# Five PSUM banks for each wide pair, decay vectors made behind the second head, sigmoids one pair later, and the first sum of values behind the weights

## The chip, the cores and the metric

The kernel runs on one core of one Trainium2 chip. The metric is the device time of one execution in microseconds; lower is better. TensorE multiplies, ScalarE (ACT) and VectorE (DVE) do everything element by element and read TensorE's results out of PSUM, GpSimd (POOL) and SyncE (SP) issue transfers.

## The reference, cut to what matters

One decoder layer of width 1024 over 512 tokens in float32: a SwiGLU block, a mixer, a second SwiGLU block, each between two RMS norms. The change lies in the mixer:

```python
u = rms_norm(h, mix_norm_pre[l])
proj = u @ w_in[l]                       # (512, 8704)
q, k, v, xr, yr, gl = jnp.split(proj, splits, axis=-1)
# q, k, v: three dilation groups x four heads x 128
for g, (window, dilation) in enumerate(((128, 1), (512, 4), (2048, 16))):
    o_g, lse_g = dilated_group_attention(q[:, :, g], k[:, :, g], v[:, :, g], ...)
alpha = jax.nn.softmax(jnp.stack(lses, axis=0), axis=0)
attn = jnp.einsum('gbsh,gbshe->bshe', alpha, jnp.stack(outs, axis=0))
attn_d = attn.reshape(B, S, 512) @ w_attn_branch[l]
...
log_a = -LRU_C * gate_a * jax.nn.softplus(-a_param)     # in the recurrence
a = jnp.exp(log_a)
...
gates = jax.nn.sigmoid(gl).reshape(B, S, 2, D_MODEL)
merged = gates[:, :, 0] * attn_d + gates[:, :, 1] * rec_d
```

## The kernel before

**Split numbers.** A float32 product is made of three passes on numbers split in a high and a low half (fp32r): `split` lets ScalarE copy the high half (L302) and VectorE subtract it for the low half (L303). Weights come by transfer into one of four `raw` buffers, issued by SyncE, and are split into one of four `w8` buffers (high and low half of 1024 columns).

**Seven products.** Most large products are done in blocks of two by two with seven products instead of eight (Strassen's scheme in Winograd's form, p1 to p7). The sums of inputs and of weights that it needs are made by VectorE: those of the weights in `w_forms` (L691 to L696), those of the inputs in `forms_of` (`early`, L667 to L669; `middle`, L673; `late`). The products of p6 and p4 read an input form in the buffer `rb`, the others one in `big`.

**The order of the work.** Each engine executes its instructions in the order that a scheduler gives them when the kernel is built; the scheduler goes by priorities (`tc.high_priority`) and by the due times that it works out. `tc.issue_after(ins)` puts an instruction behind another of the same engine in that order. An instruction that must wait holds up all behind it on its engine.

**The mixer up to the gates** has these stages, one after the other:
- the values of group 0 (`values_first`), then those of groups 1 and 2 together by seven products (`values_two`, L1236 to L1238): VectorE sums weights in place (`add`, L1221) and splits them (`form`), TensorE runs p1, p2, p5, p6, p7, p3, p4, ScalarE copies partial sums from bank to bank (L1243);
- for each of four heads, three *wide pairs*, `qk`: one `seven_wide` makes the q and the k of one group and head, 128 columns each;
- `attend` of a head, whose work stands between the next head's pairs: scores (L1340 to L1366), exponentials (L1359, L1375), `exchange` of maxima and sums between partitions by a small matmul (L1383 and L1388 on VectorE, L1386 on TensorE), weighting (L1421, L1424), transposes (L1412, copied by L1415), values (L1430, L1435), split (L1437, L1438);
- four more wide pairs for the gates' columns, each with two sigmoids behind it (L1449, L1450) that write `facc`; `facc` held the scores of the heads before;
- the product with `w_attn_branch` (L315 to L317), multiplied into `facc` (L1457);
- the recurrence, at whose head the decay vectors `sp4` and `sp8`, 128 x 8, are made of `a_param` (L1484 to L1500).

**A wide pair** (`seven_wide`) runs its products into PSUM banks of 512 columns: in each, the left half holds one part and the right half another, and the result is their sum. Sums that several results share are carried on by copying a bank to another: `move` (L784, ScalarE). `fold` copies the left half (L790, ScalarE) and adds the right (L791, VectorE); `sum_of` adds twice (L797, L798, VectorE). All of these have a high priority (`EVAC`). The banks come from a ring of five, `acc`; the pair takes four of them:

```python
        product("p2", b, False)
        fold(b, g[0])
        product("p7", v, False)
        move(b, v)
        sum_of(u[1], v, c5)
        product("p3", z, False)
        sum_of(g[1], z, c6)
        product("p4", b, False)
        fold(b, u[0])
```

A product of a wide pair is four times a matmul of 512 columns (L779) and one of 256 (L780).

Of the kernel before, what the change touches and what calls it, by code (L numbers as in the profile page):

```python
# [10 lines left out]
F32 = mybir.dt.float32  # L11
F32R = mybir.dt.float32r
AF = mybir.ActivationFunctionType
ALU = mybir.AluOpType
AX = mybir.AxisListType

P = 128
# [156 lines left out]
SMALL = {}  # L174
# [9 lines left out]
def hybrid_layer(ctx: ExitStack, tc: tile.TileContext, xT: bass.AP, xN: bass.AP, wst: bass.AP,  # L184
                 first: bass.AP, rows: bass.AP, consts: bass.AP, bias: bass.AP, out: bass.AP):
    nc = tc.nc
    DVE, ACT, PE = nc.vector, nc.scalar, nc.tensor
# [10 lines left out]
    sm = first_t[:, 512:]  # L198
# [3 lines left out]
    facc = cpool.tile([P, KC, T], F32, name="facc")  # L202
# [29 lines left out]
    state = {"g": 0, "i": 0, "off": 0, "raw": None, "ahead": AHEAD, "split": None}  # L232
# [67 lines left out]

    def split(dh, dl, src):
        state["split"] = ACT.activation(dh, src, AF.Copy).ins  # L302
        DVE.tensor_sub(dl, src, dh.bitcast(F32))  # L303

    def acc_ps():
        return psum.tile([P, T], F32, name="acc", tag="acc", bufs=5)
# [452 lines left out]
        seventh(t, w, "p4", v, False)  # L759
        u0(v)  # L760

    def seven_wide(t, w, g, u, seen=lambda ap: ap):


        b, v, z, y = (acc_ps() for _ in range(4))

        def two(ps):
            return ps[:, :HB], ps[:, HB:]

        def product(p, ps, start):  # L770
            at = t[p].at
            part, cross = ps.rearrange("q (s c) -> q s c", s=2), two(ps)[1]
            if len(at(0, 0).shape) == 3:
                part = ps.rearrange("q (s b t) -> q s b t", s=2, b=2)
                cross = cross.rearrange("q (b t) -> q b t", b=2)
            for k in range(4):
                ks = slice(k * P, (k + 1) * P)
                wh, wl = w[p][:, 0, ks], w[p][:, 1, ks]
                PE.matmul(part, wh, at(BOTH, k), start=start and k == 0, stop=False, skip_group_check=True)  # L779
                PE.matmul(cross, wl, at(0, k), start=False, stop=k == 3, skip_group_check=True)  # L780

        def move(dst, src):
            with tc.high_priority(offset=EVAC):
                ACT.activation(dst, src, AF.Copy)  # L784

        def fold(ps, dst=None):
            out = tpool.tile([P, HB], F32, name="c", tag="c", bufs=CB) if dst is None else dst
            x, y_ = two(ps) if dst is None else map(seen, two(ps))
            with tc.high_priority(offset=EVAC):
                ACT.activation(out, x, AF.Copy)  # L790
                DVE.tensor_add(out, y_, out)  # L791
            return out

        def sum_of(dst, ps, c):
            x, y_ = two(ps)
            with tc.high_priority(offset=EVAC):
                DVE.tensor_add(c, x, c)  # L797
                DVE.tensor_add(dst, seen(y_), seen(c))  # L798

        product("p1", b, True)  # L800
        move(y, b)
        product("p5", z, True)
        c5 = fold(z)
        product("p6", y, False)
        move(v, y)
        c6 = fold(y)
        product("p2", b, False)
        fold(b, g[0])
        product("p7", v, False)
        move(b, v)  # L810
        sum_of(u[1], v, c5)
        product("p3", z, False)
        sum_of(g[1], z, c6)
        product("p4", b, False)
        fold(b, u[0])

    def seven(t, w, z, g, u):

# [297 lines left out]
    for k in range(KC):  # L1116
        wh, wl, raw = wts[k]
        if k == 0:

            z = hm(0)  # L1120
# [42 lines left out]
    def rec_half():  # L1163

        return kpool.tile([P, 8, T], F32R, name="rb", tag="rb")

    with ExitStack() as mx:
        tpl = mx.enter_context(tc.tile_pool(name="attn_out", bufs=1))
        apool_cm = tc.tile_pool(name="attention", bufs=1)
# [36 lines left out]
        def values_two(steps, then):  # L1206
# [11 lines left out]
            def add(dst, x, y):  # L1218
                with tc.high_priority(offset=AHEAD):
                    for d, x_, y_ in zip(*(two_of(a) for a in (dst, x, y))):  # L1220
                        DVE.tensor_add(d, x_, y_)  # L1221

            def form(src):
                with tc.high_priority(offset=AHEAD):
                    ws = [w8(), w8()]
                    for w, half in zip(ws, two_of(src)):
                        split(w[:, 0, :], w[:, 1, :], half)
                return ws
# [22 lines left out]
            b, y, z = [aux_ps(), aux_ps()], [acc_ps(), acc_ps()], [aux_ps(), acc_ps()]  # L1251
            c5, c6 = ([facc[:, i + j, :] for j in range(2)] for i in (0, 2))
            w1, w2 = form(g0), form(g1)
            steps[0]()
            add(sd, u0, u1)
            prod("p1", w1, b, True)
            copies(y, b)
            w5 = form(sd)
# [43 lines left out]
        def pair_of(key):  # L1302

            i = order.index(key)
            if i + 1 < len(order):
                forms[order[i + 1]] = w_forms(order[i + 1])
            return forms.pop(key)
# [22 lines left out]
        def attend(hd, heads):  # L1330
# [64 lines left out]
            DVE.tensor_tensor(nm, nm, st[:, 0, 2, :], op=ALU.min)  # L1395
            e = apool.tile([P, NG, 4], F32, name="e", tag="e", bufs=2)
            DVE.tensor_tensor(e, nm[:, None, :].to_broadcast([P, NG, 4]), st[:, 0], op=ALU.subtract)
            ACT.activation(e, e, AF.Exp)
            d = apool.tile([P, NG, 4], F32, name="d", tag="d", bufs=2)
            DVE.tensor_mul(d, e, st[:, 1])  # L1400
            tot = apool.tile([P, 4], F32, name="tot", tag="tot", bufs=2)
# [33 lines left out]
                PE.matmul(on[:, :, b, :], vt[0][:, j, :], t.rearrange("q (p r) -> q p r", p=4),  # L1435
                          start=False, stop=i == 6, skip_group_check=True)
            ACT.activation(attn.hi[hd], om, AF.Copy)  # L1437
            DVE.tensor_sub(attn.lo[hd], om, attn.hi[hd].bitcast(F32))  # L1438

        for hd in range(NH):  # L1440
            attend(hd, qkvs.pop(hd))
            if hd + 1 < NH:
                qkvs[hd + 1] = qk(hd + 1)


        for c in range(0, KC, 2):
            g, u = tmp("g"), tmp("u")
            seven_wide(t, pair_of(("pair", 52 + c, 53 + c)), [g[:, h] for h in HALVES], [u[:, h] for h in HALVES])
            ACT.activation(facc[:, c, :], g, AF.Sigmoid)  # L1449
            ACT.activation(facc[:, c + 1, :], u, AF.Sigmoid, scale=-1.0)  # L1450
        apool_cm.__exit__(None, None, None)
        for c in range(KC):
            ps = acc_ps()
# [5 lines left out]
    with ExitStack() as mx:  # L1459
# [15 lines left out]
        lpool = lpool_cm.__enter__()  # L1475


        def s8(name):
            return lpool.tile([P, 8], F32, name=name)
        o, w = SMALL["ap"]  # L1480
        av = sm[:, o:o + w]
        na, ex, zz, po = (s8(n) for n in ("na", "ex", "zz", "po"))
        sp8 = s8("sp8")
        DVE.tensor_scalar(na, av, -1.0, None, op0=ALU.mult)  # L1484
        DVE.tensor_tensor(ex, av, na, op=ALU.min)
        ACT.activation(ex, ex, AF.Exp)
        DVE.tensor_scalar(zz, ex, 2.0, None, op0=ALU.add)
        DVE.reciprocal(zz, zz)
        DVE.tensor_mul(zz, zz, ex)
        DVE.tensor_mul(ex, zz, zz)  # L1490
        DVE.memset(po, 1.0 / 19.0)
        for i in (17, 15, 13, 11, 9, 7, 5, 3, 1):
            DVE.tensor_mul(po, po, ex)
            DVE.tensor_scalar(po, po, 1.0 / i, None, op0=ALU.add)
        DVE.tensor_mul(po, po, zz)
        DVE.tensor_scalar(na, na, 0.0, None, op0=ALU.max)
        DVE.scalar_tensor_tensor(po, po, 2.0, na, op0=ALU.mult, op1=ALU.add)
        DVE.tensor_scalar(sp8, po, -8.0, None, op0=ALU.mult)
        sp4 = po
        DVE.tensor_scalar(sp4, po, 4.0, None, op0=ALU.mult)  # L1500

        def ip(ap):
            return ap.rearrange("q (i p) -> q p i", p=4)
# [124 lines left out]
        for i, (what, hd) in enumerate(LRU_ORDER):  # L1628
# [9 lines left out]
            def then():  # L1638
                if i + 1 < len(LRU_ORDER):
                    prepare(LRU_ORDER[i + 1])  # L1640
# [189 lines left out]
```

## Time and profile before

| what | value |
|---|---|
| median of 3 runs | 1218.15 us (1217.16 to 1218.87) |
| the profiled execution | 1217.25 us, its span 1215.4 us |
| TensorE busy | 1200.5 us (99% of the span) |
| VectorE busy | 1030.6 us (85%) |
| ScalarE busy | 835.9 us (69%) |
| TensorE's clock | full in all 40 slices |
| HBM | 119 GB/s over the span |

All times of a trace are counted from the start of the span. In a row of a timeline the first number is the start and the second the duration in us; a bracket gives the idle time of the engine before it and what ended that. Busy times of neighbouring operations overlap a little, since a duration counts an operation to its last write. In a row of the windows, the columns are the window, its length, and the busy time and instructions of TensorE, of its weight loads, of VectorE, ScalarE and GpSimd, then TensorE's clock, the transfers' share and GB/s.

### The profile page before, as it was taken

The page shows a single profiled execution, that of the slowest core. Times are in us where ns is not written, and L with a number is a line of the kernel's source. Part 1 is how long each engine was busy: PE and PEld are TensorE (multiplying, and loading weights), DVE is VectorE, ACT ScalarE, POOL GpSimd, SP SyncE. Part 2 cuts the span into 40 slices and gives each one's busy share as a digit, 9 for nine tenths or more (in the row PEclk, how much of TensorE's full clock was granted, in tenths as well). Part 3 has the DMA queues.
Part 4 walks back from the last instruction along what each step waited for, and adds up shares of the span by engine and source line. Part 5 has one row for each costly group of instructions (what it writes and reads, how often), then busy time and mean ns, then how long its engine had stood idle before and what let it go on. Part 6 is the DMA issues. An engine that isn't in the chain of part 4 may idle for free.

```text
span 1215.4 us, 18988 instructions
## 1 busy us (share of the span) xinstructions
PE 1200.5 (99%) x7306; PEld 1073.9 (88%) x7306; DVE 1030.6 (85%) x1608; ACT 835.9 (69%) x1449; POOL 26.2 (2%) x51
## 2 busy tenths in 40 slices
PE   9999999999999999999999999999999999999997
PEld 8899999999887888888889888888899999999996
DVE  7999888989789899999867899875799888889964
ACT  7567787886575676777735898834566677877763
POOL 0000000001011000000000000000100000000000
PEclk9999999999999999999999999999999999999999
DMA  7234333434634232222323342235443343433341
GB/s 265 89 102 138 114 133 121 134 115 155 239 125 126 70 113 71 96 85 81 99 75 122 122 156 87 87 122 175 154 139 109 120 136 108 136 115 129 122 173 70
DMA packets 45818, 149.77 MB, mean 123 GB/s; under 512 B 5152, under 2 KB 8608, under 8 KB 45728
## 3 DMA queue, kind: packets, MB, share of 16 engines
q1 hardware_dynamic: 38160, 131.09, 32.5%
q0 software_dynamic: 7280, 17.30, 4.3%
q8 instruction: 57, 0.93, 0.3%
q14 instruction: 33, 0.27, 0.1%
q10 hardware_dynamic: 288, 0.17, 0.0%
HBM read 138.06 MB, written 6.29 MB: 119 GB/s over the span
## 4 chain that ended last, share of the span: by engine, by line
PE 89%; DVE 5%; ACT 3%; DMA 2%; issue 1%; SPq 0%; DVEq 0%; ACTq 0%
PE acc L729 10%; PE acc L731 10%; PE acc L730 10%; PE acc L315 7%; PE acc L317 7%; PE acc L316 7%; PE acc L779 7%; PE aux L1035 4%; PE aux L1036 4%; PE aux L1037 4%; PE acc L780 3%; DVE w L303 2%; PE acc L433 2%; PE acc L432 2%; PE acc L431 2%; DMA raw<-in_w 1%
## 5 line engine op out<-in xcount | busy, mean ns | idle before, releaser
L303 DVE TENSOR_TENSOR w<-raw,w 128x1024 fp32r<-128x1024 f32 (+1 forms) x272 | 297.5, 1098 | 36.2 <-ACT w L302 35.4
L302 ACT ACTIVATE w<-raw 128x1024 fp32r<-128x1024 f32 (+1 forms) x272 | 259.7, 959 | 92.1 <-PE acc L317 44.5
L729 PE MATMUL acc<-big,w 128*128 128x256 f32 x920 | 260.4, 283 | 0.0
L731 PE MATMUL acc<-big,w 128*128 128x256 f32 x920 | 260.3, 283 | 0.0
L730 PE MATMUL acc<-big,w 128*128 128x256 f32 x920 | 260.3, 283 | 0.0
L729 PEld LDWEIGHTS acc<-big,w 128*128 128x128 f32 x920 | 176.2, 192 | 1.9
L730 PEld LDWEIGHTS acc<-big,w 128*128 128x128 f32 x920 | 176.3, 192 | 1.7
L731 PEld LDWEIGHTS acc<-big,w 128*128 128x128 f32 x920 | 176.3, 192 | 0.0
L779 PE MATMUL acc<-big,w 128*128 128x512 f32 x320 | 115.2, 398 | 0.3 <-ACT acc L784 0.3
L780 PE MATMUL acc<-big,w 128*128 128x256 f32 x320 | 90.6, 283 | 0.0
L1035 PE MATMUL aux<-w,xf 128*128 128x512 f32 x224 | 87.5, 393 | 0.6 <-ACT w L302 0.6
L1036 PE MATMUL aux<-w,xf 128*128 128x512 f32 x224 | 87.5, 391 | 0.0
L1037 PE MATMUL aux<-w,xf 128*128 128x512 f32 x224 | 87.2, 389 | 0.0
L779 PEld LDWEIGHTS acc<-big,w 128*128 128x128 f32 x320 | 60.1, 188 | 13.7 <-ACT acc L784 0.6
L303 DVE TENSOR_TENSOR w<-s,w 128x1024 fp32r<-128x1024 f32 x51 | 62.2, 1220 | 4.9 <-ACT w L302 4.8
L780 PEld LDWEIGHTS acc<-big,w 128*128 128x128 f32 x320 | 60.5, 189 | 0.1
L315 PE MATMUL acc<-xf,w 128*128 128x512 f32 (+1 forms) x168 | 59.0, 353 | 0.0
L317 PE MATMUL acc<-xf,w 128*128 128x512 f32 (+1 forms) x168 | 58.5, 349 | 0.0
L316 PE MATMUL acc<-xf,w 128*128 128x512 f32 (+1 forms) x168 | 58.5, 349 | 0.0
L302 ACT ACTIVATE w<-s 128x1024 fp32r<-128x1024 f32 x51 | 53.8, 1056 | 6.2 <-PE acc L731 3.0
L743 ACT ACTIVATE c<-acc 128x256 f32<-128x256 f32 x74 | 28.2, 384 | 40.7 <-PE acc L731 40.7
L1035 PEld LDWEIGHTS aux<-w,xf 128*128 128x128 f32 x224 | 41.9, 188 | 9.3 <-ACT w L302 1.2
(454 smaller groups left out, 2938.6 us busy)
## 6 DMA issues: line engine op xcount, KB each, us to landing
raw<-in_w SPq DMA_DIRECT2D x232, 512.0 KB, 3.5
big<-xf POOLq DMA_DIRECT2D x6, 512.0 KB, 3.4
gains<-in_rows POOLq DMA_DIRECT2D x5, 512.0 KB, 5.7
h<-in_x SPq DMA_DIRECT2D x8, 256.0 KB, 5.3
h<-in_xn POOLq DMA_DIRECT2D x4, 512.0 KB, 6.7
kept_m<-h POOLq DMA_DIRECT2D x4, 512.0 KB, 2.9
vals<-in_w SPq DMA_DIRECT2D x4, 512.0 KB, 6.1
h<-kept_m POOLq DMA_DIRECT2D x4, 512.0 KB, 5.5
```

The costliest lines, as they stand in the source:

```text
L302: state["split"] = ACT.activation(dh, src, AF.Copy).ins
L303: DVE.tensor_sub(dl, src, dh.bitcast(F32))
L315: PE.matmul(ps, wh, xh, start=first, stop=False)
L316: PE.matmul(ps, wh, xl, start=False, stop=False)
L317: PE.matmul(ps, wl, xh, start=False, stop=last)
L729: PE.matmul(ps, wh, xh, start=start and k == 0, stop=False, skip_group_check=True)
L730: PE.matmul(ps, wh, xl, start=False, stop=False, skip_group_check=True)
L731: PE.matmul(ps, wl, xh, start=False, stop=k == 3, skip_group_check=True)
L779: PE.matmul(part, wh, at(BOTH, k), start=start and k == 0, stop=False, skip_group_check=True)
L780: PE.matmul(cross, wl, at(0, k), start=False, stop=k == 3, skip_group_check=True)
L1035: PE.matmul(ps, xh, wh, start=first and j == 0, stop=False, skip_group_check=True)
L1036: PE.matmul(ps, xh, wl, start=False, stop=False, skip_group_check=True)
```

## The change

Four edits:
- `seven_wide` takes five banks instead of four, in the order b, z, y, v, o. The move behind p7 goes to the fifth, `o`, and p4 accumulates there; before, both used b, which `fold` of `g[0]` reads.
- `seven_wide` calls a function `then` behind that move, in ScalarE's order. The gate pairs use it to put a pair's two sigmoids behind the third move of the next pair; those of the last pair follow at the end.
- The decay vectors are made in `decay`, called once, after the second head's `attend`: its Exp stands behind that head's last Exp in ScalarE's order, its VectorE operations behind the split of that head's output. They live in a pool that lasts until the recurrence.
- In `values_two` the first sum (`add(sd, u0, u1)`) is put behind the low half of the last weights split before it (`state["low"]`).

```diff
     def split(dh, dl, src):
         state["split"] = ACT.activation(dh, src, AF.Copy).ins
-        DVE.tensor_sub(dl, src, dh.bitcast(F32))
+        state["low"] = DVE.tensor_sub(dl, src, dh.bitcast(F32)).ins
...
-    def seven_wide(t, w, g, u, seen=lambda ap: ap):
-        b, v, z, y = (acc_ps() for _ in range(4))
+    def seven_wide(t, w, g, u, seen=lambda ap: ap, then=lambda: None):
+        b, z, y, v, o = (acc_ps() for _ in range(5))
...
         def move(dst, src):
             with tc.high_priority(offset=EVAC):
-                ACT.activation(dst, src, AF.Copy)
+                return ACT.activation(dst, src, AF.Copy).ins
...
         product("p7", v, False)
-        move(b, v)
+        moved = move(o, v)
         sum_of(u[1], v, c5)
+        with tc.issue_after(moved):
+            then()
         product("p3", z, False)
         sum_of(g[1], z, c6)
-        product("p4", b, False)
-        fold(b, u[0])
+        product("p4", o, False)
+        fold(o, u[0])
...
+    decays = [s8(n, kpool) for n in ("po", "sp8")]
+
+    def decay(pool):
+        o, w = SMALL["ap"]
+        av = sm[:, o:o + w]
+        na, ex, zz = (s8(n, pool) for n in ("na", "ex", "zz"))
+        po, sp8 = decays
+        DVE.tensor_scalar(na, av, -1.0, None, op0=ALU.mult)
+        DVE.tensor_tensor(ex, av, na, op=ALU.min)
+        ACT.activation(ex, ex, AF.Exp)
+        DVE.tensor_scalar(zz, ex, 2.0, None, op0=ALU.add)
...
+        for i in (17, 15, 13, 11, 9, 7, 5, 3, 1):
+            DVE.tensor_mul(po, po, ex)
+            DVE.tensor_scalar(po, po, 1.0 / i, None, op0=ALU.add)
...
             w1, w2 = form(g0), form(g1)
+            low = state["low"]
             steps[0]()
-            add(sd, u0, u1)
+            with tc.issue_after(low):
+                add(sd, u0, u1)
             prod("p1", w1, b, True)
...
-            ACT.activation(e, e, AF.Exp)
+            state["exp"] = ACT.activation(e, e, AF.Exp).ins
...
-            DVE.tensor_sub(attn.lo[hd], om, attn.hi[hd].bitcast(F32))
+            state["low"] = DVE.tensor_sub(attn.lo[hd], om, attn.hi[hd].bitcast(F32)).ins
 
         for hd in range(NH):
             attend(hd, qkvs.pop(hd))
+            if hd == 1:
+                with tc.issue_after(state["exp"]), tc.issue_after(state["low"]):
+                    decay(apool)
             if hd + 1 < NH:
                 qkvs[hd + 1] = qk(hd + 1)
 
+        two = []
+
+        def gate():
+            if two:
+                c, g, u = two.pop()
+                ACT.activation(facc[:, c, :], g, AF.Sigmoid)
+                ACT.activation(facc[:, c + 1, :], u, AF.Sigmoid, scale=-1.0)
 
         for c in range(0, KC, 2):
             g, u = tmp("g"), tmp("u")
-            seven_wide(t, pair_of(("pair", 52 + c, 53 + c)), [g[:, h] for h in HALVES], [u[:, h] for h in HALVES])
-            ACT.activation(facc[:, c, :], g, AF.Sigmoid)
-            ACT.activation(facc[:, c + 1, :], u, AF.Sigmoid, scale=-1.0)
+            seven_wide(t, pair_of(("pair", 52 + c, 53 + c)), [g[:, h] for h in HALVES], [u[:, h] for h in HALVES],
+                       then=gate)
+            two.append((c, g, u))
+        gate()
...
-        na, ex, zz, po = (s8(n) for n in ("na", "ex", "zz", "po"))
...
+        sp4, sp8 = decays
```

More of the change, by code (lines that the diff above doesn't have):

```diff
@@ L1165, in rec_half, with s8 @@
         return kpool.tile([P, 8, T], F32R, name="rb", tag="rb")
+    def s8(name, pool):
+        return pool.tile([P, 8], F32, name=name)
+    decays = [s8(n, kpool) for n in ("po", "sp8")]
[8 more added lines that the diff above has]
+        DVE.tensor_scalar(zz, ex, 2.0, None, op0=ALU.add)
+        DVE.reciprocal(zz, zz)
+        DVE.tensor_mul(zz, zz, ex)
+        DVE.tensor_mul(ex, zz, zz)
+        DVE.memset(po, 1.0 / 19.0)
+        for i in (17, 15, 13, 11, 9, 7, 5, 3, 1):
+            DVE.tensor_mul(po, po, ex)
+            DVE.tensor_scalar(po, po, 1.0 / i, None, op0=ALU.add)
+        DVE.tensor_mul(po, po, zz)
+        DVE.tensor_scalar(na, na, 0.0, None, op0=ALU.max)
+        DVE.scalar_tensor_tensor(po, po, 2.0, na, op0=ALU.mult, op1=ALU.add)
+        DVE.tensor_scalar(sp8, po, -8.0, None, op0=ALU.mult)
+        DVE.tensor_scalar(po, po, 4.0, None, op0=ALU.mult)
     with ExitStack() as mx:
@@ L1475, in hybrid_layer @@
         lpool = lpool_cm.__enter__()
[L1478 to L1481, printed above, removed]
-        na, ex, zz, po = (s8(n) for n in ("na", "ex", "zz", "po"))
[L1483 to L1500, printed above, removed]
+        sp4, sp8 = decays
         def ip(ap):
```

## The prediction

> **What bounds the kernel now.** I read the page first, then the windows over the mixer's attention, then the timeline of each engine at every place where TensorE's starts lie further apart than its steady pitch.
>
> ```profile
> PE 1200.5 (99%) x7306; PEld 1073.9 (88%) x7306; DVE 1030.6 (85%) x1608; ACT 835.9 (69%) x1449; POOL 26.2 (2%) x51
> PE 89%; DVE 5%; ACT 3%; DMA 2%; issue 1%; SPq 0%; DVEq 0%; ACTq 0%
> ```
> ```profile
> 359.00:412.00 53.00, 50.52 (x225) 41.26 (x224) 47.63 (x50) 33.33 (x45) 7.93 (x16) 1.00 0.39 115
> 519.00:557.00 38.00, 38.00 (x239) 33.63 (x238) 36.44 (x79) 26.32 (x62) 0.00 (x0) 1.00 0.26 87
> ```
>
> TensorE is the bound: 1200.5 us of 1215.4, and 89% of the chain. The change adds and removes no matmul, so all it can win are TensorE's waits between the values (359 us) and the end of the gate pairs (612 us), 253 us in all. VectorE is nearly as full there (in the window of the third head 36.44 of 38 us); what is taken from TensorE's waits must not come back as VectorE's. The engine orders of the two kernels, both built, are the same outside this stretch, so a gain there should shift the rest unchanged.
>
> **Part 1, the first sum of values later.** TensorE's timeline, then VectorE's:
>
> ```profile
> 368.27 0.39 PE L1236 MATMUL aux<-w,big 128*128 128x512 f32 x1
> 369.82 0.50 PE L1237 MATMUL aux<-w,big 128*128 128x512 f32 x1 [1.16 <-DVE w L303]
> 381.51 0.61 PE L1236 MATMUL aux<-w,rb 128*128 128x512 f32 x2
> 383.44 0.50 PE L1237 MATMUL aux<-w,rb 128*128 128x512 f32 x1 [1.32 <-DVE w L303]
> ```
> ```profile
> 366.27 1.23 DVE L1221 TENSOR_TENSOR vals<-vals 128x1024 f32<-128x1024 f32 x1 [1.10 <-DMA vals<-in_w]
> 367.41 1.22 DVE L303 TENSOR_TENSOR rb<-ts,rb 128x1024 fp32r<-128x1024 f32 x1
> 368.55 4.62 DVE L303 TENSOR_TENSOR w<-raw,w 128x1024 fp32r<-128x1024 f32 x4
> 382.17 2.35 DVE L303 TENSOR_TENSOR w<-vals,w 128x1024 fp32r<-128x1024 f32 x2
> 386.71 1.22 DVE L303 TENSOR_TENSOR big<-ts,big 128x1024 fp32r<-128x1024 f32 x1
> ```
>
> Between 369.82 and 381.51 TensorE does 51 steps, 0.229 us each. So the first wait (369.82 - 368.27 = 1.55) costs 1.32, the second (the second matmul of the pair at 381.51 starts 0.23 later, 383.44 - 381.74 = 1.70) costs 1.47; each adds 0.10, since the matmul behind a wait takes 0.50 instead of 0.39. Both are waits for a low half of weights. The cause is one sum (L1221) that stands at the head of VectorE's queue and waits 1.10 us for its transfer.
>
> In the changed order the sum stands behind the four low halves of the 368.55 row, and its place is taken by p5's low half (the 386.71 row), whose inputs are long made. VectorE was free at 366.27 - 1.10 = 365.17; its pitch is 367.41 - 366.27 = 1.14; the first weights' low half starts after two steps, at 367.45 instead of 368.55. The first wait shrinks by 1.10. p6's first low half (382.17 now) comes twelve steps later, at 381.1, done at 382.3; but TensorE now finishes p5 before p6 and asks for it only at its 73rd matmul, 368.72 + 72 x 0.229 = 385.2. The second wait goes: 1.57. What is late next is p7: its input's low half comes seven steps and one short one (0.6) behind, 389.6 to 390.8, and is wanted at 368.72 + 96 x 0.229 = 390.7: with the refill I count 0.3. Gain 1.10 + 1.57 - 0.3 = **2.4 us**; bounds 1.1 (the second wait turns into others) and 2.9.
>
> **Part 2, five banks.** The last gate pair, TensorE, ScalarE, VectorE; and the first pair's wait:
>
> ```profile
> 598.15 0.28 PE L780 MATMUL acc<-big,w 128*128 128x256 f32 x1
> 599.51 0.51 PE L779 MATMUL acc<-rb,w 128*128 128x512 f32 x1 [1.08 <-ACT acc L784]
> 602.33 0.28 PE L780 MATMUL acc<-big,w 128*128 128x256 f32 x1
> 602.93 0.50 PE L779 MATMUL acc<-big,w 128*128 128x512 f32 x1 [0.32 <-ACT acc L784]
> 606.09 0.40 PE L316 MATMUL acc<-attn,w 128*128 128x512 f32 x1
> 606.52 0.50 PE L779 MATMUL acc<-rb,w 128*128 128x512 f32 x1
> ```
> ```profile
> 593.41 1.28 ACT L1486 ACT_TABLE_LOAD   x1
> 597.05 1.28 ACT L1449 ACT_TABLE_LOAD   x1
> 598.35 0.63 ACT L1449 ACTIVATE facc<-g 128x512 f32<-128x512 f32 x1
> 598.88 0.58 ACT L784 ACTIVATE acc<-acc 128x512 f32<-128x512 f32 x1
> 601.76 0.63 ACT L302 ACTIVATE w<-raw 128x512 fp32r<-128x512 f32 x1 [1.48 <-DMA raw<-in_w]
> 602.29 0.58 ACT L784 ACTIVATE acc<-acc 128x512 f32<-128x512 f32 x1
> 605.88 0.58 ACT L784 ACTIVATE acc<-acc 128x512 f32<-128x512 f32 x1 [0.54 <-DVE g L791]
> ```
> ```profile
> 598.41 0.17 DVE L1493 TENSOR_TENSOR po<-po,ex 128x8 f32<-128x8 f32 x1
> 598.61 0.17 DVE L1494 TENSOR_SCALAR po<-po 128x8 f32<-128x8 f32 x1
> 605.37 0.42 DVE L791 TENSOR_TENSOR g<-acc,g 128x256 f32<-128x256 f32 x1
> 607.84 0.41 DVE L798 TENSOR_TENSOR g<-acc,c 128x256 f32<-128x256 f32 x1
> ```
> ```profile
> 418.13 0.28 PE L780 MATMUL acc<-big,w 128*128 128x256 f32 x1
> 418.47 0.50 PE L779 MATMUL acc<-rb,w 128*128 128x512 f32 x1
> ```
>
> p4 waits at 606.52 for the move at 605.88, and ScalarE stood idle 0.54 before that move: it writes bank b, which VectorE's fold of g0 (605.37 + 0.42) still reads. TensorE loses 0.43 - 0.23 + 0.10 = 0.30. Such a wait stands before p4 in six of the sixteen wide pairs, from 418.47 (0.34 - 0.12 + 0.10 = 0.32) to 606.52, 1.88 us together. With a fifth bank the move needs only p7 and ScalarE, so it starts 0.46 to 0.54 earlier, more than the 0.2 or so that TensorE stood still. One of the six also had ScalarE busy with weights; in the changed order those stand behind the move. I take **1.5**; bounds 0.8 and 1.9. What is late next is ScalarE itself, finishing a 1.06 us weight copy when p7 ends.
>
> **Part 3, sigmoids behind a copy of the next pair, and no Exp between them.** ScalarE loads a table for Exp at 593.41 and one back for Sigmoid at 597.05; p6 of the last pair waits for the move that comes behind load and sigmoid (598.88): 599.51 - 598.15 = 1.36, less 0.12, plus 0.11: 1.35. In the changed order one load is left, behind a move. p7 of the same pair waits for the move at 602.29, which stands behind a weight copy that waited 1.48 for its transfer: 0.60 - 0.12 + 0.10 = 0.58. That copy now stands behind the last pair's third move and its two sigmoids, some 8 us after its buffer is free. Together 1.93; the deferred load delays the fold of g0 of the pair it lands in, whose bank the next p1 needs about 1 us later by my count, so I count it at nothing; if that cover is gone it costs up to the load's 1.28. Gain **1.9**, bounds 0.6 and 2.2.
>
> **Part 4, the order of the first head's softmax** is made anew by the scheduler, since all around it moves.
>
> ```profile
> 447.74 0.28 PE L780 MATMUL acc<-big,w 128*128 128x256 f32 x1
> 448.90 0.38 PE L1386 MATMUL aux<-xch,cst 128*128 128x32 f32 x2 [0.88 <-DVE xch L1383]
> ```
>
> TensorE waits 1.16 - 0.12 = 1.04 here for the exchange of maxima. In the changed order this matmul stands over a pair later, 1.7 us or so behind the point at which its input should be ready. Gain **0.9**; bounds -0.5 (the exchange, or another in the new order, waits anyway) and 1.0.
>
> **Part 5, the decay vectors in the third head's stage.** Thirty small VectorE operations and one Exp leave the gate pairs. They hid behind TensorE there except for the load of part 3. Now they stand singly between VectorE's other work while head 2's pairs run.
>
> ```profile
> 577.32 0.15 DVE L1403 TENSOR_TENSOR tot<-tot,d 128x4 f32<-128x4 f32 x1
> 577.38 1.22 DVE L303 TENSOR_TENSOR w<-s,w 128x1024 fp32r<-128x1024 f32 x1
> ```
> ```profile
> DVE c L791 <- ACT c L790: 0.8, 1, 0.8
> DVE w L303 <- ACT w L302: 0.5, 1, 0.5
> DVE qk L791 <- ACT qk L790: 0.5, 1, 0.5
> ```
>
> The second fence is VectorE's waits in 519 to 557. A small operation between large ones holds the queue for 577.38 - 577.32 = 0.06; in a chain, one needing the one before, it takes 598.61 - 598.41 = 0.20. The changed order alternates them with other work, so I take a little over the first, 0.08: 30 x 0.08 = 2.4 us, against 1.8 of waiting that can take them. **0.6 us** is lost; bounds 0 and 30 x 0.20 - 1.8 = 4.2. The Exp finds its table loaded and costs ScalarE one small step. The vectors' reader comes after 612 us.
>
> For small waits that any new order makes I take **0.5**, bounds 0 and 1.5, from the refill of 0.1 and waits of 0.2 that stand in six of sixteen pairs now.
>
> **Sum.** 2.4 + 1.5 + 1.9 + 0.9 - 0.6 - 0.5 = 5.6 us. The profiled execution took 1217.25 (span 1215.4), so 1211.65; the median shown, 1218.15, lies 0.9 above it, so **1212.6**. Two in a thousand, 2.4 us, is about what a measurement of this kernel can tell from no change.
>
> **Rivals.** *The small operations cost their full length* (0.12). If VectorE takes nothing up before a small operation has ended, each costs 0.20: 4.2 us net in place of 0.6, gain 6.7 - 4.2 - 0.5 = 2.0, **1216.2**. Against it: the rows 577.32 and 577.38. The Trainium skill, "VectorE: DVE Perf Modes", section "The DRAIN you can't avoid", says that the next operation waits until the pipe is empty, and advises fewer operations. By that rule this rival holds; the rows above disagree with it, at 0.06 against a duration of 0.15.
>
> *Exchanges take the waits over* (0.10). Each head has two; TensorE, which executes in order, stood still at one of eight. With TensorE ahead of VectorE, if four of the eight wait 0.98 (0.88 and the refill), part 4 is gone and three are added: 6.7 - 0.9 - 2.9 - 1.1 = 1.8, **1216.4**. For it: VectorE is as full as the second window says.
>
> *Slower: the bank of p5 comes round too soon* (0.08). With five of five banks per pair, p5 of the next pair takes the very bank z that p3 just filled, so it waits for VectorE's sum of g1 (607.84 + 0.41 = 608.25), 1.73 after p4's start at 606.52. Two products run from 599.51 to 602.33 + 0.12, 1.41 each, so p5 follows p4's start by p4 and p1, 2.82: the slack is 1.09. From there each tenth by which the sum comes later is a tenth lost in each of fifteen pairs. It takes 0.55 a pair, sums 1.65 later, to eat 5.6 and 2.4 more: **1220.6**. One more weight half (1.22) and a few decay operations ahead of the sum would do it; against it, the sums go ahead of weights in the queue.
>
> **How the numbers follow.** The forecast has 0.70. Its best end is 2.9 + 1.9 + 2.2 + 1.0 = 8.0, 1210.1; I set the low end at 1209.9. The first two rivals end near 1216.4; a little past them, at 1216.8, the range leaves out the slower rival (0.08) and the worse ends of the first two (about 0.1): 1209.9 to 1216.8. Faster by over 0.2%: nearly all of the forecast (0.68) and some of the first two rivals (0.10), 0.78; within 0.2%: the rest of these, 0.13; slower: 0.09.
>
> **What would show it.** Right: no wait over 0.4 us of TensorE on L303 in the values; no gap before p4; ScalarE's moves never idle behind L791; one table load in the gate pairs; the exchange of head 0 without a wait; VectorE's waits in head 2 down to almost none. Wrong, if TensorE's waits between 359 and 612 still add up to over 8 us, if p5 of a pair waits on L798, or if the exchanges wait.

## The result, and the profile after

The changed kernel takes 1211.81 us (median of 6 runs, 1210.72 to 1212.27) where the kernel before takes 1218.03 (6 runs, 1217.16 to 1218.87): a ratio of 0.9948, 95% interval 0.9935 to 0.9961, 6.2 us faster. The forecast was 1212.6. The sum came out nearly right, in part by luck: one of its terms, and a part of another, goes back to another edit than the one it stood under, and a loss of about 1 us or a little more was not in it at all.

The profiled execution took 1211.87 (span 1210.1). First the page's busy times and chain.

```profile
PE 1199.2 (99%) x7306; PEld 1073.7 (89%) x7306; DVE 1029.0 (85%) x1608; ACT 832.4 (69%) x1447; POOL 26.1 (2%) x51
PE 88%; DVE 6%; ACT 3%; DMA 2%; issue 1%; DVEq 0%
```

These shares hardly moved. The waits did: TensorE's between 359 and 612 us, before (first fence) and after (second). The columns are engine, tile and line, then what was waited for, the total in us, how often, and the longest.

```profile
PE aux L1237 <- DVE w L303: 2.5, 2, 1.3
PE acc L779 <- ACT acc L784: 1.4, 2, 1.1
PE aux L1386 <- DVE xch L1383: 0.9, 1, 0.9
```
```profile
PE aux L1372 <- DVE qk L791: 0.5, 1, 0.5
```

All three kinds are gone, and one new one of 0.5 has come. (Line numbers have moved: the second and third matmul of a step of the values, L1237 and L1238, are now L1267 and L1268, the exchange L1418, the sigmoids L1486 and L1487.) The values and the new wait, TensorE; then VectorE in front of the values:

```profile
368.23 0.39 PE L1266 MATMUL aux<-w,big 128*128 128x512 f32 x1
368.62 0.50 PE L1267 MATMUL aux<-w,big 128*128 128x512 f32 x1
...
418.17 0.28 PE L780 MATMUL acc<-big,w 128*128 128x256 f32 x1
418.90 0.49 PE L1372 MATMUL aux<-qk 128*128 128x128 f32 x2 [0.46 <-DVE qk L791]
```
```profile
366.21 1.22 DVE L303 TENSOR_TENSOR rb<-ts,rb 128x1024 fp32r<-128x1024 f32 x1
367.35 4.62 DVE L303 TENSOR_TENSOR w<-raw,w 128x1024 fp32r<-128x1024 f32 x4
```

The weights' low halves start at 367.35 (forecast 367.45). Of the first wait 368.62 - 368.23 - 0.23 = 0.16 is left; the second is gone.

To see where gains arise, and where they are given back, I took the start of the n-th matmul in the trace of before, less that in another trace, both counted from the first matmul at 361 us. This "lead", at points named by the time of before, with the gain of the medians (the kernels are described below):

| kernel | 410, values done | 457 | 509, two heads done | 578, third head done | 612, gates done | 705 | 841, recurrence done | gain of the median |
|---|---|---|---|---|---|---|---|---|
| changed | 2.38 | 3.25 | 3.71 | 4.26 | 6.99 | 6.86 | 6.12 | 6.22 |
| only_sum | 2.63 | 1.69 | 1.67 | 1.60 | 1.68 | 1.41 | 1.41 | 0.98 |
| only_banks | -0.03 | 1.72 | 2.39 | 2.82 | 3.11 | 3.11 | 3.11 | 2.86 |
| only_decay | -0.59 | -0.53 | -1.29 | -1.65 | 0.59 | 0.51 | -0.23 | -1.45 |
| only_sig | 0.41 | 0.38 | 0.20 | 0.28 | 0.02 | 0.02 | 0.02 | 0.04 |
| no_sum | -0.67 | 1.07 | 1.53 | 1.61 | 4.34 | 4.23 | 3.49 | 2.84 |
| no_banks | 2.41 | 1.35 | 0.56 | 0.22 | 2.54 | 2.12 | 1.38 | 1.76 |
| no_decay | 2.43 | 3.05 | 3.83 | 4.41 | 5.84 | 5.74 | 5.00 | 4.82 |
| decay_twice | 2.45 | 2.99 | 4.46 | 2.00 | 4.33 | 3.74 | 2.12 | 2.64 |
| aligned | 2.60 | 3.08 | 3.84 | 4.55 | 7.44 | 7.44 | 7.44 | 7.93 |
| shift_128 | 2.40 | 2.96 | 3.29 | 3.66 | 6.22 | 5.63 | 4.01 | 4.08 |
| only_decay_aligned | -0.10 | -0.21 | -1.22 | -1.65 | 0.58 | 0.58 | 0.58 | 0.94 |
| no_sig_aligned | 2.61 | 3.39 | 3.95 | 4.67 | 6.99 | 6.99 | 6.99 | 7.20 |

The lead at 841 us agrees with the gain of the medians to 0.7 us, but for only_decay, 1.2 off. Behind it single executions differ by up to 2 us in waits for weights (only_banks' lead falls from 3.11 to 1.03 by the last matmul, the changed kernel's from 6.12 to 5.33), so one profile's last stage says little. Where two kernels take heads in another order, a point within the heads can be off by some tenths.

The changed kernel's lead is largest at the end of the gate pairs, 6.99. Then, where no instruction was changed, it shrinks by 0.87, of which 0.74 in the recurrence. That and the waits of each edit are what the experiments are for.

### The profile page after: what moved, and what is told of

It reads as the page before. It is cut to its first block, busy times and chain, and to the rows that moved or that the text cites. A ratio compares the mean times of both kernels' runs of the same rounds, so it can differ in the third digit from the quotient of the medians.

```text
span 1210.1 us, 18990 instructions
## 1 busy us (share of the span) xinstructions
PE 1199.2 (99%) x7306; PEld 1073.7 (89%) x7306; DVE 1029.0 (85%) x1608; ACT 832.4 (69%) x1447; POOL 26.1 (2%) x51
## 4 chain that ended last, share of the span: by engine, by line
PE 88%; DVE 6%; ACT 3%; DMA 2%; issue 1%; DVEq 0%
PE acc L729 9%; PE acc L731 9%; PE acc L730 9%; PE acc L779 8%; PE acc L315 7%; PE acc L317 7%; PE acc L316 7%; PE acc L780 4%; PE aux L1037 3%; PE aux L1038 3%; PE aux L1039 3%; DVE w L303 2%; DMA raw<-in_w 2%; PE acc L433 2%; PE acc L432 2%; PE acc L431 2%
```

## Experiments: one edit at a time

Each of the four edits alone, on the kernel before.

**only_sum**

```
-            add(sd, u0, u1)
+            with tc.issue_after(low):
+                add(sd, u0, u1)
```

> The kernel before with one edit alone: the first sum of values stands behind the low halves of the second weights. Theory 1 (the parts add up: TensorE is the bound, and a wait that goes is a gain that stays): the two waits in the values at 368 and 382 us, 1.55 and 1.70, shrink to under 0.5 together; lead at the end of the values 2.4 to 2.6 us, and the time 2.4 us below before. Rival 2 (VectorE is the hidden pace-setter): the same lead at the end of the values, but VectorE, as full as before, gives over 1 us of it back in the heads by new waits of TensorE on VectorE's low halves; the time falls by under 1.4 us.

1217.02 us (11 runs), ratio 0.9990, interval 0.9981 to 0.9999: 1.0 us, not 2.4. The lead is as forecast at the end of the values, 2.63, and 0.94 less at 457. TensorE, VectorE and ScalarE of this kernel at the first pair of head 0:

```profile
415.50 0.28 PE L780 MATMUL acc<-big,w 128*128 128x256 f32 x1
416.72 0.50 PE L779 MATMUL acc<-rb,w 128*128 128x512 f32 x1 [0.94 <-ACT acc L784]
```
```profile
414.44 1.22 DVE L303 TENSOR_TENSOR w<-s,w 128x1024 fp32r<-128x1024 f32 x1
415.57 0.42 DVE L791 TENSOR_TENSOR qk<-acc,qk 128x256 f32<-128x256 f32 x1
```
```profile
416.08 0.58 ACT L784 ACTIVATE acc<-acc 128x512 f32<-128x512 f32 x1 [1.47 <-DVE qk L791]
```

Before, p4 started 0.34 after the last matmul of p7 (418.13 to 418.47); now it starts 1.22 after it. TensorE has come 2.6 us closer to VectorE, whose fold still holds bank b, and the move of that pair stands 1.47 behind it. Rival 2 holds: the gain is real, and in this kernel the next shared bank takes 0.9 of it back.

**only_banks**

```
-        b, v, z, y = (acc_ps() for _ in range(4))
+        b, z, y, v, o = (acc_ps() for _ in range(5))
...
-        move(b, v)
+        move(o, v)
...
-        product("p4", b, False)
-        fold(b, u[0])
+        product("p4", o, False)
+        fold(o, u[0])
```

> The kernel before with one edit alone: five banks in each wide pair, the move of the partial sums going to a fifth bank. Theory 1 (waits add up): the six waits before p4 go and nothing else does; 1.5 us faster, at most 1.9; the two waits of the last gate pairs (1.36 and 0.60 us, behind the table loads) stay. Rival 2: ScalarE, finishing a weight copy when p7 ends, moves no earlier, or the extra bank makes the next pair's p5 wait for VectorE's sum of g1; within 0.5 us of before, or slower, with gaps before p5.

1215.14 us (7 runs), ratio 0.9976, interval 0.9964 to 0.9987: 2.9 us, nearly twice what was expected. TensorE's waits from 407 to 612 us in this kernel, and then the exchange of head 0 on TensorE and VectorE:

```profile
PE acc L779 <- ACT acc L784: 1.5, 2, 1.1
```
```profile
453.56 0.30 PE L1386 MATMUL aux<-xch,cst 128*128 128x32 f32 x2
```
```profile
453.22 0.18 DVE L1383 TENSOR_TENSOR xch<-stn,cst 128x32 f32<-128x32 f32 x1
```

The two waits left are those of the last gate pairs. The exchange's wait of 0.9 is gone without any other edit: with the fifth bank the exchange stands at 453.56 (448.90 before), and TensorE does not wait for it. The scheduler makes this order with the fifth bank alone, so Part 4 of the forecast is a result of the banks.

**only_sig**

```
-        move(b, v)
+        moved = move(b, v)
         sum_of(u[1], v, c5)
+        with tc.issue_after(moved):
+            then()
...
-            ACT.activation(facc[:, c, :], g, AF.Sigmoid)
-            ACT.activation(facc[:, c + 1, :], u, AF.Sigmoid, scale=-1.0)
+            two.append((c, g, u))
+        gate()
```

> The kernel before with one edit alone: each gate pair's sigmoids stand behind the next pair's move. Its decay vectors are still made in the gate pairs, and with them three table loads (Sigmoid, Exp, Sigmoid). Theory 1: the table loads, and not the place of the sigmoids, made the wait of 1.36 us, so it stays or turns up at another product; the wait of 0.60 at p7 may go since its weight copy moves. 0 to 0.6 us faster. Rival 2 (the place of the sigmoids is what the waits of the gate pairs came from): both waits go without the decay vectors being moved, 1.5 to 2 us faster.

1217.96 us (11 runs), ratio 0.9999, interval 0.9991 to 1.0008: nothing. But the lead shows a gain that is lost again: 0.28 at 578 us, 1.01 at 605, 0.02 at 612. TensorE's waits from 552 to 615 us, then the second of them and the move that it waits for:

```profile
PE acc L779 <- ACT acc L784: 1.8, 2, 1.1
```
```profile
605.86 0.50 PE L779 MATMUL acc<-rb,w 128*128 128x512 f32 x1 [1.07 <-ACT acc L784]
```
```profile
605.23 0.58 ACT L784 ACTIVATE acc<-acc 128x512 f32<-128x512 f32 x1 [1.02 <-DVE g L791]
```

With the decay vectors' Exp beside the sigmoids the table is loaded three times, as before. Of the two waits of the gate pairs, the one at p6 is shorter (0.72 idle, 1.08 before) and the one at p7 is gone. A wait of 1.07 has come in front of p4, whose move must wait for VectorE's fold of the shared bank b; it takes the gain back. So theory 1 holds: the wait turns up at another product.

**only_decay**: `decay(apool)` behind the second head as in the change, its two vectors taken from `kpool`, the old code removed.

> The kernel before with one edit alone: the decay vectors' 30 small VectorE operations and their Exp stand behind the second head, in the third head's stage. Theory 1: the gate pairs keep one table load in place of three; the wait of 1.36 us at the last pair's p6 goes (gain 1.2 to 1.4), the one of 0.60 at p7, which is a weight copy waiting for its transfer, stays; the small operations cost 0 to 0.6 us in the third head; 0.8 to 1.4 us faster. Rival 2 (small operations hold VectorE for their full 0.17 to 0.20 us): 30 x 0.20 less VectorE's waits there, 1.8, so TensorE loses about 4 us in the third head and the time rises by 2 to 3 us.

1219.45 us (11 runs), ratio 1.0012, interval 1.0004 to 1.0021: slower. The stages say otherwise for the gate pairs (from -1.65 to 0.59, a gain of 2.2, more than expected, since the wait at p7 goes too). But 0.6 is lost in the values, 1.1 from 457 to 578 and 0.74 from 705 to 841. A loss in the heads was expected, though not its size. About half of it stands ahead of the first small operation, which starts at 514.87 in this kernel: the lead is -0.52 at 486 and -1.05 at 513 us. In between TensorE's order differs from that of before. The losses in the values and in the recurrence were in neither theory.

The four alone gain 0.98 + 2.86 + 0.04 - 1.45 = 2.4, together 6.2. Here the edits do not add up.

## Experiments: one edit taken out

**no_sum**, the changed kernel with `add(sd, u0, u1)` at its old place.

> The changed kernel without the edit of the first sum. Theory 1 (the parts add up): the two waits in the values are back, 1.3 and 1.5 us; the time is 2.4 to 2.6 us above the changed kernel's, so 3.5 to 4 us below before. Rival 2 (slack is shared: what one part gains, another would have given): under 1.4 us above the changed kernel.

1215.38 us (7 runs), ratio 0.9973, interval 0.9962 to 0.9984. TensorE's waits from 359 to 612 us:

```profile
PE aux L1267 <- DVE w L303: 2.8, 2, 1.5
PE aux L1417 <- DVE xch L1414: 0.2, 1, 0.2
```

Within the changed kernel the edit is worth (0.9973 - 0.9948) x 1218 = 3.0 us; alone it was worth 1.0. The leads at 841 us say 2.6 and 1.4.

The fifth bank is not what makes the difference. From 410 to 509 us the changed kernel loses 0.87 against no_sum, and only_sum lost 0.96 against before: with five banks the first matmul of the scores waits (418.90 in the changed kernel; no_sum has no such wait), with four p4 does. Of the 1.2 between 2.6 and 1.4, 0.4 arises in the values, where this kernel's two waits are 2.8 together against 2.5 before, and the rest behind 509 us; what made it there was not shown.

**no_banks**

```
-        b, z, y, v, o = (acc_ps() for _ in range(5))
+        b, v, z, y = (acc_ps() for _ in range(4))
+        o = b
```

> The changed kernel with four banks in each wide pair, the move going back into the bank of g0's fold. Theory 1: waits before p4 are back, 1.5 to 1.9 us in all, and the time is that much above the changed kernel's, 4.3 to 4.7 us below before. Rival 2: with the sigmoids and the decay vectors elsewhere, ScalarE and VectorE are early enough that p4 does not wait: within 0.7 us of the changed kernel.

1216.46 us (11 runs), ratio 0.9989, interval 0.9980 to 0.9998: (0.9989 - 0.9948) x 1218 = 5.0 us are lost, three times the expectation. The waits from 407 to 516 us (one line further down, since this version has a line more):

```profile
PE acc L780 <- ACT acc L785: 1.0, 1, 1.0
PE aux L1419 <- DVE xch L1416: 0.9, 1, 0.9
```

They are only_sum's wait in front of p4 and the exchange. The lead of 2.41 from the values falls to 1.35 at 457 and 0.22 at 578: first by what only_sum lost there, then by 1.13, which only_decay lost between the same points (1.12). With five banks the move of the decay vectors costs 0.35 there (no_decay, below). So the fifth bank removes its own waits and most of this loss; the sum's loss of 0.9 it does not remove, as no_sum shows.

**no_decay**, the changed kernel with `decay(lpool)` called where the old code was.

> The changed kernel with the decay vectors made where they were, beside the gate pairs. Theory 1: the Exp brings three table loads back into the gate pairs, a wait of 1.0 to 1.4 us with them; the small operations leave the third head, where VectorE's waits come back to 1.8 us; 0.6 to 1.4 us above the changed kernel. Rival 2 (30 small operations in the third head cost several us that other gains cover): 2 us or more below the changed kernel.

1213.40 us (5 runs), ratio 0.9962, interval 0.9948 to 0.9975: (0.9962 - 0.9948) x 1218 = 1.7 us are lost (1.1 by the leads at 841 us; the two intervals overlap). So the move of the decay vectors is worth 1 to 1.7 us in the company of the others. From 578 to 612 the lead grows by 1.43, against 2.73 in the changed kernel; from 457 to 578 by 1.36 against 1.01. So the move costs 0.35 from 457 to 578 us and brings 1.3 in the gate pairs. The lead of no_decay grows by 1.14 up to 605 us and does not fall behind it: what the sigmoids' move gains here stays with five banks, where only_sig lost it.

**decay_twice**, a second, unused set of decay vectors ahead of the first: 30 more small operations of VectorE and an Exp.

```
+    spare_decays = [s8(n, kpool) for n in ("po2", "sp82")]
...
+                    decay(apool, spare_decays)
                     decay(apool)
```

> The changed kernel with a second set of decay vectors, used by nothing, made right beside the first in the third head's stage: 30 more small VectorE operations and one more Exp. If a small operation holds VectorE for 0.08 us: 30 x 0.08 = 2.4 us more work for an engine that has few waits left there, so 1 to 2.4 us above the changed kernel, in waits of TensorE on VectorE between 510 and 550 us. If it holds VectorE for its full 0.20 us: 30 x 0.20, 4 to 6 us above. If the third head still has slack on VectorE's side: 0 to 0.5 us.

1215.58 us (11 runs), ratio 0.9978, interval 0.9969 to 0.9987: (0.9978 - 0.9948) x 1218 = 3.7 us slower than the changed kernel. That is above what 0.08 us each allows and below 0.20 each. But the lead shows two losses: one up to the third head's end, and 1.62 in the recurrence, where neither set is computed. The recurrence had to be understood first.

## Experiments: where the recurrence lost

The kernels that lose nothing between 705 and 841 us are before, only_sum, only_banks and only_sig. Those that lose 0.74 hold two decay vectors in `kpool`; decay_twice, which loses 1.62, holds four. Each is 32 bytes a partition and stands ahead of the halves of the input (rb). In the built programs rb lies at byte 147200 of a partition in the first group, at 147264 in the second, at 147328 in decay_twice; the attention output and the recurrence's tile behind it are shifted alike. TensorE's groups that read rb in the recurrence, 706 to 830 us, in the changed kernel (busy us, mean ns):

```profile
L315 PE MATMUL acc<-rb,w 128*128 128x512 f32 x36 | 14.2, 394 | 0.0
L317 PE MATMUL acc<-rb,w 128*128 128x512 f32 x36 | 14.1, 392 | 0.0
L316 PE MATMUL acc<-rb,w 128*128 128x512 f32 x36 | 14.0, 388 | 0.0
```

Before, all three rows have 389. Three explanations stood: the addresses, a slower clock after a denser stage, and decay_twice's instructions.

**aligned**, the changed kernel with the two vectors in a stretch of SBUF that holds the first weights at the start and nothing later. Instructions and their order stay; only the addresses return to those of before.

```
-    decays = [s8(n, kpool) for n in ("po", "sp8")]
+    decays = [first_t[:, 8 * i:8 * i + 8] for i in range(2)]
```

> The changed kernel, all engines' orders unchanged, with the two decay vectors (64 bytes a partition) kept in a stretch of SBUF that is dead by then, not in a tile of their own, so that the halves of the input, the attention output and the recurrence's tile lie at the addresses they had before (147200 and 163584 in place of 147264 and 163648). Theory 1 (where these tiles lie sets TensorE's pitch): the recurrence's matmuls run at 0.2267 us a step, as in the kernel before, not at 0.2267 to 0.2298; the 0.74 us lost between 705 and 841 us comes back, with 0.2 to 0.5 in the values and the output projection; 0.8 to 1.3 us below the changed kernel. Rival 2 (the chip slows TensorE because the stage before it is denser): the pitch stays, and the time with it.

**shift_128**, the same with an unused tile that shifts rb and what follows by 128 bytes.

```
+    pad = kpool.tile([P, 32], F32, name="pad")
+    DVE.memset(pad[:, :1], 0.0)
```

> The kernel 'aligned' with an unused 128 bytes a partition ahead of the input's halves, so that these tiles lie 128 bytes further on; all engines' orders the same but for one small memset. Theory 1 (addresses): steps of 0.229 and 0.237 us by turns wherever these tiles are read, 1.6 us lost in the recurrence, some 2.5 us above 'aligned'. Rival 2 (the 0.237 us in the run with two sets of decay vectors came of their 30 instructions): the same time as 'aligned'.

aligned: 1210.20 us (5 runs, 1210.05 to 1210.68), ratio 0.9940, interval 0.9926 to 0.9953. shift_128: 1214.05 us (7 runs), ratio 0.9971, interval 0.9960 to 0.9982. The two differ by 3.9 us, by addresses and one small memset alone; by the leads, 2.2 of it arises from 612 to 841 us. The windows from 706 to 830 us of before, the changed kernel, aligned and shift_128, in this order:

```profile
706.00:830.00 124.00, 124.00 (x549) 102.71 (x548) 102.83 (x135) 89.89 (x115) 1.06 (x2) 1.00 0.31 100
```
```profile
706.00:830.00 124.00, 124.00 (x546) 102.08 (x545) 100.80 (x132) 84.96 (x111) 1.06 (x2) 1.00 0.32 110
```
```profile
706.00:830.00 124.00, 124.00 (x549) 102.68 (x548) 100.44 (x131) 85.56 (x111) 1.05 (x2) 1.00 0.35 114
```
```profile
706.00:830.00 124.00, 124.00 (x542) 101.34 (x541) 101.62 (x132) 85.04 (x110) 1.05 (x2) 1.00 0.33 103
```

TensorE is never idle in any of the four and its clock is 1.00; it does 549, 546, 549 and 542 matmuls in the same time. Seven matmuls fewer of 549 in 124 us are 1.58 us, the 1.62 that decay_twice lost at the same addresses. aligned is as dense as the changed kernel in the stage before and loses nothing, so the second explanation falls; shift_128 has no second set and is as slow in the recurrence as decay_twice, so the third falls too. The rows of aligned for one of the groups above, and of shift_128 for it and for a group that reads `big`, which none of these kernels moves:

```profile
L315 PE MATMUL acc<-rb,w 128*128 128x512 f32 x36 | 14.0, 389 | 0.0
```
```profile
L315 PE MATMUL acc<-big,w 128*128 128x512 f32 x85 | 33.1, 389 | 0.0
L315 PE MATMUL acc<-rb,w 128*128 128x512 f32 x36 | 14.2, 395 | 0.0
```

From start to start, the 108 matmuls of this tile are 226.7 ns apart on average in before and aligned, 228.9 in the changed kernel, 233.3 in shift_128. Those that read `big` keep 226.7 to 227.1 in all four. Two sets of decay vectors against one can now be compared at equal addresses: from 457 to 578 us decay_twice's lead falls by 0.99 where shift_128's grows by 0.70. That is 1.69 us for 30 small operations, 0.06 each, if they alone made it; the scheduler's order differs there too.

**only_decay_aligned**, only_decay with the vectors in the dead stretch.

> The kernel before with the decay vectors made in the third head's stage, the vectors kept where they move no other tile. Theory 1: the loss of that edit alone was the shifted tiles and the third head; without the shift it gains 2.2 us in the gate pairs and loses 0.4 to 0.8 in the third head, so 1 to 1.8 us faster than before. Rival 2 (the loss is the small operations'): at or above the time before.

1217.19 us (11 runs), ratio 0.9996, interval 0.9988 to 1.0005: no difference that can be told, less than theory 1 gave, and rival 2's "at the time before" lies inside the interval. The leads bear out theory 1 by stage: the recurrence keeps its lead of 0.58, the values lose 0.1 in place of 0.6, the gate pairs gain 2.2. From 457 to 578 us 1.4 is lost, more than expected, and here again over half of it (from -0.17 at 486 to -0.99 at 513) ahead of the first small operation.

**no_sig_aligned**, aligned with `gate()` right behind its own pair.

> The kernel 'aligned' with each gate pair's sigmoids right behind their own pair. Theory 1: with one table load left, the sigmoids' place is worth the wait at p7 (0.58 us in the kernel before) at most: 0 to 0.6 us above 'aligned'. Rival 2: without the move, the one table load lands in front of a move again, 1.0 to 1.4 us above.

1210.93 us (5 runs), ratio 0.9943, interval 0.9930 to 0.9955, against aligned's 0.9940. The leads give the sigmoids' move 7.44 - 6.99 = 0.45 us, inside theory 1's range but not where it put it: p7's wait does not come back, and the 0.45 arises between 578 and 598 us, around the one table load. The medians, 0.7 apart with intervals that overlap, do not contradict this and do not prove it. aligned is the fastest of all kernels here.

## Why the prediction was right, and where it was not

**Part 1** (2.4 us): the lead at the end of the values is 2.38. The first wait shrank by 1.55 - 0.39 = 1.16 (1.10 taken), the second went, and the wait of 0.3 at p7 did not come; the shift told of below took about 0.2 back (aligned has 2.60). What the step did not see is that VectorE takes some 0.9 of it back a few products later, at p4 with four banks and at the scores with five.

**Parts 2 and 4** (1.5 and 0.9): only_banks gains 3.1 from the values' end to 612 us, where the two terms have 2.4 together, and both come from the fifth bank. For the new order of the first head's softmax, which the forecast put down to all that moves around it, the banks are enough. ScalarE's waits in front of the move, before and after, 407 to 612 us:

```profile
ACT acc L784 <- DVE qk L791: 2.4, 5, 0.6
ACT acc L784 <- DVE g L791: 0.5, 1, 0.5
```
```profile
ACT acc L784 <- PE acc L780: 8.4, 9, 2.4
ACT acc L784 <- DVE e L1437: 1.1, 1, 1.1
ACT acc L784 <- DVE xch L1415: 1.1, 1, 1.1
ACT acc L784 <- ACT c L790: 0.2, 1, 0.2
```

No move stands behind L791 any more, as forecast. From 410 to 509 us only_banks gains 2.4, the changed kernel 1.33: behind 418.17 the first matmul of the scores waits (418.90 - 418.17 - 0.12 = 0.61). That is the term for new small waits, 0.5, in one place, and it comes of the sum.

**Part 3** (1.9): from 578 to 612 us the lead grows by 2.73, but not all of this is Part 3. The lead is 4.69 at 598 us, in front of the two waits, 6.05 at 601 and 6.69 at 605: 2.0 for the two, so the size was right. The 0.4 ahead of 598 stood in no term, and the 0.3 behind 605 is p4's wait at 606.52, of Part 2. The loads go because the Exp goes, as forecast. But the wait at p7 was put down to a weight copy that the sigmoids' move would shift, and only_decay, which leaves the sigmoids where they were, loses both waits as well (-1.38 at 598, 0.62 at 605). Once the loads are gone, the sigmoids' move adds 0.45, in front of 598. The deferred load was counted at nothing. The changed kernel's ScalarE:

```profile
587.06 1.28 ACT L1486 ACT_TABLE_LOAD   x1
588.36 0.63 ACT L1486 ACTIVATE facc<-g 128x512 f32<-128x512 f32 x1
```

One load is left, and it ends before the next move is due: no wait of TensorE is listed there.

**Part 5** (a loss of 0.6): measured 0.35 from 457 to 578 us, no_decay against the changed kernel. VectorE in the changed kernel, and its waits from 514 to 552 us:

```profile
526.91 0.16 DVE L1190 TENSOR_SCALAR po<-po 128x8 f32<-128x8 f32 x1
526.98 0.42 DVE L798 TENSOR_TENSOR qk<-acc,c 128x256 f32<-128x256 f32 x1
527.32 0.15 DVE L1189 TENSOR_TENSOR po<-po,ex 128x8 f32<-128x8 f32 x1
527.39 0.42 DVE L797 TENSOR_TENSOR c<-acc,c 128x256 f32<-128x256 f32 x1
```
```profile
DVE qk L791 <- ACT qk L790: 0.7, 2, 0.4
DVE w L303 <- ACT w L302: 0.2, 1, 0.2
DVE attn L1470 <- ACT attn L1469: 0.2, 1, 0.2
```

A small operation holds the queue for 0.07, about the 0.08 taken, and its duration is 0.16: the first rival falls. (The Trainium skill, "VectorE: DVE Perf Modes", section "The DRAIN you can't avoid", says that the next operation does not start until the pipe is empty, but also that one "that is not held starts earlier". The rows here, 0.07 after the start of an operation of 0.16, go with the second, as those of before did.) VectorE's waits shrank from 1.8 to 1.1, not to "almost none". Without the fifth bank the move costs 1.1 to 1.4 (no_banks, only_decay, only_decay_aligned), about half of it or more ahead of the first small operation. No wait of TensorE over 0.3 is listed there, so why four banks make the move dearer is not shown.

**The other rivals.** No exchange waits in the changed kernel, so they did not take the waits over. No p5 waits for L798: the z bank's slack was enough. (The forecast's 1.09 is a little small: its rows, 599.51 to 602.45, give 1.47 for each of the two products and not 1.41, and so a slack of about 1.2.)

**The step that failed** is the sentence that a gain before 612 us should shift the rest unchanged because the engines' orders are the same there. The orders are the same and the pitch is not. The diff takes two small tiles from `kpool`; the forecast read them as a question of time and not of place. It cost 0.74 us in the recurrence and, with what aligned gains elsewhere, 1.3 in the leads at 841 us and 1.6 in the medians (1211.81 against 1210.20; the intervals of their ratios overlap, but the leads show the 0.74 directly). That the forecast still came within 0.8 us is in part luck. Part 1 and Part 3 had the right size. Parts 2, 4 and 5 with the small waits brought 1.88 from 410 to 578 us and 0.3 at the last p4, 2.2 in place of 1.3, and 0.4 came around the table load; against these 1.3 stands the loss of 0.87 behind 612 us.

## What to carry to other kernels

A gain can be given back at the next place where one engine waits for another. What only_sig gained by 605 us went at the next shared bank and stayed where the bank was not shared; of what the sum gained, 0.9 went with four banks and with five. So look for the place where a lead shrinks before an edit is dropped, and test the edit in the company of the others: alone the four gave 2.4 us, together 6.2. When an edit that changes an activation function's place helps, ask which function's table loads went, since the edit beside it may have been enough. After any change of what a pool holds, compare the matmuls per us of stages that were not touched.

## What of the hardware was not expected

The place of an operand in SBUF changed TensorE's pitch. With rb and the recurrence's tile at 147200 and 163584 (multiples of 256 bytes) matmuls that read rb are 226.7 ns apart; 64 bytes further on 228.9, with durations of 388 to 394 ns by turns; 128 bytes further on 233.3, with TensorE's instructions the same and in the same order and its clock at 1.00. Matmuls in the same stretch that read `big`, which was not moved, stay at 226.7 to 227.1. No engine waits and nothing is listed as a wait: it shows in the mean duration of the groups and the count of matmuls in a window. Why this is so, and what other positions would give, was not settled; three were tried.
